# Attention scores on one core: 16 KB load runs, whole tiles to one evacuating engine, and earlier transposes

## The chip, the cores and the metric

The kernel runs on one core of a Trainium2 chip. The metric is device time in microseconds (us). The profile's span of one execution is about 1.8 us shorter than that time (204.96 with 203.2).

## The reference

```python
# q, k: float32 [8, 8, 512, 64]; result: float32 [8, 8, 512, 512]
scale = 1.0 / np.sqrt(q.shape[-1])
return (np.einsum('bhqd,bhkd->bhqk', q, k) * scale).astype(np.float32)
```

It reads 16.78 MB and writes 67.11 MB. That is 83.89 MB for 1.07 billion multiply-adds.

## The kernel before

The work is cut in four units of two batches. Each unit loads keys and queries, casts them to bf16, transposes them on TensorE so that the head dimension lies on partitions, and computes eight store tiles of 2 MB. The queries go into a tile whose other half is zero, so that one matmul over 128 partitions serves one of two heads.

```python
raw_pool = ctx.enter_context(tc.tile_pool(name="raw", bufs=4))    # 8 KB a partition each
bf_pool = ctx.enter_context(tc.tile_pool(name="bf", bufs=5))
t_pool = ctx.enter_context(tc.tile_pool(name="t", bufs=2))
out_pool = ctx.enter_context(tc.tile_pool(name="out", bufs=5))    # 16 KB a partition each
tpsum_pool = ...  # 2 PSUM tiles for transposes; psum_pool: 3 for scores
# ... load_and_cast(v): four 1 MB loads a unit, in 8 KB runs
            for x in range(2):
                xf = raw_pool.tile([P, R * D], f32, name="xf")
                nc.sync.dma_start(out=xf, in_=src[v, x])
# ... transpose(v, kb, qb): after eight transposes into tp, both engines take half of it
            for x in range(2):
                for h in range(2):
                    copy = (nc.vector.tensor_copy, nc.scalar.copy)[h]
                    copy(out=kT[half(h), x * N:(x + 1) * N, :, j0:j0 + 8],
                         in_=tp[half(x)].rearrange("d j (n h m) -> d h n m j", n=N, h=2)[:, h])
# ... scores(v, c, kT, qz): 4 x (two matmuls, one eviction on ScalarE or VectorE), one 2 MB store
# ... the order
    ts = {0: transpose(0, *cast[0])}
    for v in range(UNITS):
        for c in range(C):
            scores(v, c, *ts[v])
            if c == C // 2 - 1 and v + 1 < UNITS:
                ts[v + 1] = transpose(v + 1, *cast[v + 1])
```

## Time and profile before

| | before |
|---|---|
| time, median | 204.4 us |
| span of the profiled run | 203.2 us |
| TensorE / VectorE / ScalarE busy | 52% / 63% / 52% |
| mean rate over the span | 413 GB/s |
| mean rate of slices 1 to 7 (loads) | 422 GB/s |
| mean rate of slices 9 to 37 (stores) | 430 GB/s |

Read the DMA row of the slices first (the prediction shows it): it is full from the second slice on, so the question for any change is whether it lets the queue of transfers run empty, or makes a byte cheaper. Then read how far ahead of the transfers the stores are issued. The view of the output tensor gives the times from issue to landing, the list of waits what the two evacuating engines wait for (total us, times, longest):

```profile
DMA to landing us min/median/max: 12.9/20.5/23.2
```

```profile
ACT kT L99 <- DVE kT L99: 11.6, 11, 4.6
ACT qz L110 <- DVE qz L110: 11.4, 15, 1.6
```

A landing of 20.5 us is four store tiles of 4.9 us each in the queue, a landing of 12.9 us fewer than three. ScalarE loses 23.0 us in all to VectorE on the transposed tiles, but neither engine is the bound.

### The profile page before, as it was taken

What the parts mean: (1) busy time and instruction counts of PE and PEld (TensorE: products, weight loads), DVE (VectorE), ACT (ScalarE), POOL (GpSimd) and SP (SyncE); (2) the same over time, 40 slices, a digit from 0 to 9 for tenths busy, and PEclk for the clock granted to TensorE, in tenths of its full rate; (3) what the DMA queues carried; (4) which work ended last, traced back from release to release, by engine and by line L of the source; (5) the groups of instructions that cost most, each with busy time, mean ns of one, the idle gap of its engine ahead of it and who ended that gap; (6) DMA issues with size and microseconds to landing.
All of it is one profiled execution on the core that took longest, in us unless ns stands there. A gap on an engine that the chain in (4) does not pass through costs nothing.

```text
span 203.2 us, 1530 instructions
## 1 busy us (share of the span) xinstructions
PE 105.0 (52%) x512; PEld 48.5 (24%) x512; DVE 128.3 (63%) x131; ACT 104.8 (52%) x131; POOL 34.8 (17%) x21
## 2 busy tenths in 40 slices
PE   0033579873388535979555938545455755610000
PEld 0033334332352213533122413112121211200000
DVE  3793778997769989779678889444444444440000
ACT  2317668866676867688384787333333333330000
POOL 8957777706000000000000000000000000000000
PEclk9999999999559999699988699997975597575555
DMA  6999999999999999999999999999999999999990
GB/s 226 427 411 429 421 426 423 419 424 426 432 435 426 435 423 423 439 429 426 435 432 423 435 426 432 435 423 439 429 424 435 426 429 435 429 429 439 423 419 35
DMA packets 6919, 83.98 MB, mean 413 GB/s; under 512 B 768, under 2 KB 768, under 8 KB 768
## 3 DMA queue, kind: packets, MB, share of 16 engines
q1 hardware_dynamic: 6912, 83.89, 97.3%
q8 instruction: 4, 0.07, 0.1%
q14 instruction: 3, 0.02, 0.0%
HBM read 16.78 MB, written 67.11 MB: 413 GB/s over the span
## 4 chain that ended last, share of the span: by engine, by line
DMA 42%; DVE 17%; PE 15%; ACT 13%; issue 1%; SPq 0%; ACTq 0%
DMA out_dram<-o 38%; PE ps L121 9%; DVE o L60 8%; ACT o L58 6%; DMA xf<-in_q_dram 4%; DVE kT L99 4%; ACT kT L99 4%; PE tp L105 4%; DVE qz L110 3%; PE tp L94 3%; ACT qz L110 2%; DVE xb L76 2%; ACT xb L76 1%; SPq L71 0%; ACTq L58 0%
## 5 line engine op out<-in xcount | busy, mean ns | idle before, releaser
L121 PE MATMUL ps<-kT,qz 128*128 128x512 bf16 x256 | 82.3, 450 | 38.2 <-ACT o L58 30.6
L60 DVE TENSOR_SCALAR o<-ps 128x1024 f32<-128x1024 f32 x64 | 77.5, 1223 | 36.2 <-DMA out_dram<-o 22.1
L58 ACT ACTIVATE o<-ps 128x1024 f32<-128x1024 f32 x64 | 63.2, 1022 | 40.7 <-DMA out_dram<-o 34.7
L121 PEld LDWEIGHTS <-qz 128*128 128x128 bf16 x256 | 27.3, 109 | 86.7 <-issue 70.4
L99 ACT COPY kT<-tp 64x512 bf16<-64x512 bf16 x32 | 18.4, 579 | 15.6 <-DVE kT L99 11.6
L110 DVE COPY qz<-tp 64x512 bf16<-64x512 bf16 x32 | 21.5, 686 | 6.5 <-PE tp L105 6.2
L76 POOL CAST xb<-xf 128x2048 bf16<-128x2048 f32 x12 | 22.7, 1893 | 15.5 <-PE tp L94 7.0
L94 PE MATMUL tp<-identity,xb 128*128 128x128 bf16 x128 | 12.5, 261 | 24.0 <-ACT kT L99 11.1
L110 ACT COPY qz<-tp 64x512 bf16<-64x512 bf16 x32 | 18.2, 579 | 12.1 <-DVE qz L110 11.4
L99 DVE COPY kT<-tp 64x512 bf16<-64x512 bf16 x32 | 21.3, 684 | 5.0 <-PE tp L94 4.4
L105 PE MATMUL tp<-identity,xb 128*128 128x128 bf16 x128 | 12.4, 263 | 12.6 <-ACT kT L99 7.3
L94 PEld LDWEIGHTS <-xb 128*128 128x128 bf16 x128 | 10.9, 121 | 27.5 <-issue 16.3
L105 PEld LDWEIGHTS <-xb 128*128 128x128 bf16 x128 | 11.0, 121 | 16.6 <-issue 15.4
L85 POOL MEMSET qz<- 64x4096 bf16 x3 | 11.5, 3830 | 0.1
L76 DVE CAST xb<-xf 128x2048 bf16<-128x2048 f32 x2 | 7.2, 3604 | 3.7 <-DMA xf<-in_k_dram 2.6
L76 ACT CAST xb<-xf 128x2048 bf16<-128x2048 f32 x2 | 3.8, 1897 | 6.1 <-DMA xf<-in_k_dram 6.0
L85 DVE MEMSET qz<- 64x2048 uint32 x1 | 1.8, 1765 | 1.2 <-PEq L158 1.2
L76 ACT ACT_TABLE_LOAD x1 | 1.3, 1283 | 0.7 <-PEq L158 0.7
masks.py:199 POOL TENSOR_SCALAR_AFFINE_SELECT identity<-identity 128x128 bf16<-128x128 bf16 x1 | 0.3, 292 | 0.1
masks.py:197 POOL MEMSET identity<- 128x128 bf16 x1 | 0.2, 204 | 0.3 <-POOLq L158 0.3
L158 POOL MEMSET const-float32-0.0<- 128x1 f32 x1 | 0.1, 103 | 0.2 <-issue 0.2
L158 POOL MEMSET const-bfloat16-1.0<- 128x1 bf16 x1 | 0.1, 111 | 0.0
(2 smaller groups left out, 0.2 us busy)
## 6 DMA issues: line engine op xcount, KB each, us to landing
out_dram<-o SPq DMA_DIRECT2D x32, 2048.0 KB, 20.5
xf<-in_k_dram SPq DMA_DIRECT2D x8, 1024.0 KB, 7.9
xf<-in_q_dram SPq DMA_DIRECT2D x8, 1024.0 KB, 8.4
```

Of the source, the lines that this page charges most:

```text
L58: nc.scalar.mul(out=dst, in_=src, mul=scale)
L60: nc.vector.tensor_scalar(out=dst, in0=src, scalar1=scale, scalar2=None, op0=mybir.AluOpType.mult)
L76: copy(out=xb[:, :, x, :], in_=xf.rearrange("p (j d) -> p j d", j=R))
L85: engine.memset(qz[half(h), :, :, (1 - h) * U:(2 - h) * U], 0.0)
L94: nc.tensor.transpose(out=tp[:, j, :], identity=identity, in_=kb[:, j0 + j].rearrange("p x d -> p (x d)"))
L99: copy(out=kT[half(h), x * N:(x + 1) * N, :, j0:j0 + 8], in_=tp[half(x)].rearrange("d j (n h m) -> d h n m j", n=N, h=2)[:, h])
L105: nc.tensor.transpose(out=tp[:, i, jj, :], identity=identity, in_=qb[:, RO * jj + i0 + i].rearrange("p x d -> p (x d)"))
L110: copy(out=qz[half(h), i0:i0 + IW, x * N:(x + 1) * N, h * U:(h + 1) * U] .rearrange("d i n (m jj) -> d i n m jj", jj=JJ), in_=tp[half(x)]. ...
L121: nc.tensor.matmul(out=ps[:, w, :], lhsT=qz[:, i + w, c, :], rhs=kT[:, c].rearrange("d m j -> d (m j)"), start=True, stop=True)
L158: nc = _bacc.Bacc("TRN2", target_bir_lowering=False, num_devices=1)
```

## The change

Its intent: half as many loads with runs twice as long; no waiting of the two engines on each other in a transposed tile; and the second unit's transposes early, while loads still fill the queue. The larger load buffers take the room of one output buffer.

```diff
-    q_r = q.rearrange("(v x) g (m j) d -> v x (g m) (j d)", x=2, j=R)
+    q_r = q.rearrange("(v b) g (m j) d -> v (b g m) (j d)", b=2, j=R)
 # ... k_r, out_r alike
-    raw_pool = ctx.enter_context(tc.tile_pool(name="raw", bufs=4))
+    raw_pool = ctx.enter_context(tc.tile_pool(name="raw", bufs=3))
-    out_pool = ctx.enter_context(tc.tile_pool(name="out", bufs=5))
+    out_pool = ctx.enter_context(tc.tile_pool(name="out", bufs=4))
 # ... load_and_cast
-            for x in range(2):
-                xf = raw_pool.tile([P, R * D], f32, name="xf")
-                nc.sync.dma_start(out=xf, in_=src[v, x])
+            xf = raw_pool.tile([P, 2, J * D], f32, name="xf")
+            nc.sync.dma_start(out=xf, in_=src[v])
 # ... the evacuation of a transposed tile
+    def rearrange(tp, pattern, dst):
+        nonlocal n_tp
+        copy = (nc.vector.tensor_copy, nc.scalar.copy)[n_tp % 2]
+        n_tp += 1
+        for s in range(2):
+            src = tp[half(s)].rearrange(pattern, n=N, h=2)
+            for h in range(2):
+                copy(out=dst(s, h), in_=src[:, h])
 # ... the order
-            if c == C // 2 - 1 and v + 1 < UNITS:
+            if n == (1 if v == 0 else N // 2 - 1) and v + 1 < UNITS:
```

## The prediction

> **What bounds the kernel now.** I read the page's slices first (its part 2), then the queue table (part 3), then the windows at the hand-over from loads to stores and at the end, then the chain of waits. The slices decide most of it:
>
> ```profile
> span 203.2 us, 1530 instructions
> ...
> PE   0033579873388535979555938545455755610000
> ...
> DVE  3793778997769989779678889444444444440000
> ACT  2317668866676867688384787333333333330000
> ...
> DMA  6999999999999999999999999999999999999990
> GB/s 226 427 411 429 421 426 423 419 424 426 432 435 426 435 423 423 439 429 426 435 432 423 435 426 432 435 423 439 429 424 435 426 429 435 429 429 439 423 419 35
> ...
> q1 hardware_dynamic: 6912, 83.89, 97.3%
> q8 instruction: 4, 0.07, 0.1%
> ```
>
> A slice is 203.2/40 = 5.08 us. The DMA row stands at 9 from the second slice to the last but one, while no compute engine is full for long. So the transfers are the bound, and not by a chain of waits but by bytes: 83.89 MB must pass (16.78 read, 67.11 written). The GB/s row gives two rates. Slices 1 to 7 are loads: mean 2956/7 = 422 GB/s. Slices 9 to 37 are stores: mean 430. Loads take 16.78/0.422 = 39.8 us, stores 67.11/0.430 = 156.1 us, together 195.9 us; the other 7 us of the span are the first issue, the ramp and the end. The end is worth a look in the windows view (length, busy time of PE, PEld, DVE, ACT, POOL, clock, DMA share, GB/s):
>
> ```profile
> 38.00:40.00 2.00, 1.71 (x8) 0.60 (x7) 2.00 (x2) 1.46 (x3) 1.62 (x1) 1.00 1.00 414
> 40.00:42.00 2.00, 1.85 (x7) 0.57 (x6) 1.97 (x3) 1.85 (x2) 0.27 (x1) 1.00 0.99 381
> ...
> 199.00:200.00 1.00, 0.00 (x0) 0.00 (x0) 0.00 (x0) 0.00 (x0) 0.00 (x0) 0.50 0.04 16
> 200.00:201.00 1.00, 0.00 (x0) 0.00 (x0) 0.00 (x0) 0.00 (x0) 0.00 (x0) 0.50 0.08 33
> ```
>
> A DMA share of 0.04 to 0.08 is about one engine of sixteen: for the last 2 to 3 us one engine finishes alone. Adding up the two-microsecond windows, 16.66 MB have moved by 42.0 us, so the loads end at 42.3 us; the hand-over costs no more than the 381 shows. From there a 2.10 MB store tile keeps the queue busy 2.10/0.430 = 4.9 us. The kernel is slower only if a tile is not issued by the time its predecessor's data is out.
>
> How near that is, the chain of waits tells (start, length, what):
>
> ```profile
> 85.33 0.02 SPq L125
> ...
> 85.38 12.88 DMA out_dram<-o
> ...
> 107.93 20.24 DMA out_dram<-o
> ```
>
> The eleventh tile was issued at 85.3 us and landed 12.9 us later. Its own data is 4.9 us and I allow 1.3 us for issue and receipt (an estimate), so some 6.5 us of stores were still queued ahead: that is the smallest lead anywhere. The next, at 107.9 us, had over 13 us.
>
> **What the Trainium skill says.** "DMA: Bandwidth & Descriptors", Where 436 GB/s comes from, puts the ceiling of one core at 435 GB/s; the stores' 430 agrees, so no rearrangement of engines can make them faster. Its section Why small descriptors are slow counts about 3 extra cycles per packet, where a cycle carries 32 bytes, and 32 bytes of descriptor. For an 8 KB run, if it goes as one packet, that is 3 on 256 cycles and 32 on 8192 bytes. The loads are indeed 1.8% below the stores here, but direction and size are mixed in this difference. "PSUM — Partial Sum Buffer", PSUM bank collisions raise a hardware error, has two engines reading the same bank and quadrant kept apart by a dependency. This trace agrees (timeline, start and length first):
>
> ```profile
> 23.34 0.68 DVE L110 COPY qz<-tp 64x512 bf16<-64x512 bf16 x1 [1.10 <-PE tp L105]
> ...
> 24.06 0.58 ACT L110 COPY qz<-tp 64x512 bf16<-64x512 bf16 x1 [1.21 <-DVE qz L110]
> ...
> 27.44 1.87 PE L105 MATMUL tp<-identity,xb 128*128 128x128 bf16 x16 [0.86 <-ACT qz L110]
> ```
>
> ScalarE begins its copy from the tile only when VectorE's 0.68 us on the same half are over, so a tile's four copies take three in a row, some 2.1 us.
>
> **The change part by part.**
>
> Loads: 16 of 1 MB in 8 KB runs become 8 of 2 MB in 16 KB runs; same bytes. An estimate from the skill's section: 39.8 us x (3/256 - 3/512 + 32/8192 - 32/16384) = 0.3 us saved. If the whole gap of 422 to 430 came from run length, 39.8 - 39.0 = 0.8 us. All of this lies on the bound. The load buffers hold 3 x 2 MB instead of 4 x 1 MB, so more is queued; the fourth load goes when the first is cast, at about 12 us (landed 8.0, VectorE's cast 3.8 us), and three loads keep the queue until 2.3 + 3 x 4.97 = 17.2 us. No gap.
>
> First tile: the casts start when the whole 2 MB are there, so transposes start near 12 us instead of 10.0. VectorE and ScalarE now each take four copies of their own tile, 4 x 0.69 = 2.75 us and 4 x 0.58 = 2.3 us, side by side. A pair of tiles costs one group of eight transposes (0.6 to 1.0 us) plus 2.75, so 3.4 to 3.8 us, against 4.0 before (18.32 to 22.29 us in the timeline). Gain 0.2 to 0.6 us a pair, 1 to 2 us a unit, all beside the transfers. The number of copies, transposes and matmuls and the shapes are unchanged: the output of the query copy is now in runs of 4 elements, but its source was strided already, so I keep 0.69 and 0.58 us. By my sum the first store is ready at 34 us (before: 35.7), the second at 37; neither matters before 42.3.
>
> Output buffers 5 to 4: (4 x 8 + 5 x 16) KB = (3 x 16 + 4 x 16) KB per partition, so they pay for the larger loads. This takes up to one tile, 4.9 us, from the lead.
>
> Second unit's transposes after two store tiles instead of four: now only stores 1 and 2 cover them, until 42.3 + 2 x 4.9 = 52.1 us. The built order on VectorE after these two is 8 key copies, 1 eviction, 4 query copies, 1 eviction (third tile), 4 query copies, 2 evictions (fourth). With 0.69 and 1.22 us each, 0.6 us per transposed group, and some 2 us in which TensorE's order makes it wait for a free output bank: third tile at 37 + 12 x 0.69 + 2 x 1.22 + 2 = 49.7 us, needed by 52.1 - 1.2 = 50.9. Fourth: + 4 x 0.69 + 2 x 1.22 + 1 = 55.9, needed by 55.8. So the margin at these two is about nothing: 0 to 2 us of empty queue. For the third unit the same sum gives the eleventh tile at 88 to 90 us, needed at 90.1; for the fourth, 2 to 4 us of margin.
>
> Sum: 204.4 - 0.3 (run length) + 0.4 (empty queue, an estimate weighted over 0 to 2 us) = 204.5 us.
>
> **The rivals.** (1) Nothing at all: the transfers are full either way, 203.9 to 204.4 us. For it: the DMA row, and equal bytes; I hold it likeliest. (2) The queue runs dry where transposes now cover only two tiles, or where one fewer output buffer is queued: 205 to 208 us. For it: the sum above has little margin, and in slices 10 and 11 before the TensorE clock fell to 0.5, which makes a group of eight transposes 1.0 us instead of 0.6. Against: the two engines now evacuate side by side without waiting on each other, and the early transposes lie beside loads. (3) Longer runs help loads by more than the estimate, or the ramp of the first 3 us is shorter as the first two megabytes go by one issue: 203.2 to 203.8 us. Against a gain over 2%: it would need 200.3 us, under the 195.9 us of data plus the start and the tail, which the change leaves alone.
>
> **Range and chances.** Low end 203.3: rival 3 with no gap. High end 206.3: about 2 us of gaps. Slower by 2% (over 208.5) needs 4 us of gaps, twice my worst sum; 0.05. Faster by 2%: 0.02. Within: 0.93.
>
> **What will show it.** The DMA row at 9 from slice 1 to 38 says rival 1; a 7 or 8, or GB/s below 400, in slices 9 to 11 (50 to 58 us) or 17 (88 us) says rival 2. The GB/s of slices 1 to 7 above 425 shows the run length worth something; 430 would show that length, not direction, was the gap. Copies of 0.69 and 0.58 us, and no ScalarE copy waiting for VectorE, show the evacuation step right. The smallest store landing time should fall from 12.9 us to 6 to 10. The prediction is wrong if the query copies grow with their 4-element runs (0.3 us on 32 copies per engine would empty the queue), or if a load waits for a cast.

## The result, and the profile after

The changed kernel takes 204.52 us (204.16 to 204.69, 4 runs) against 204.40 (204.25 to 204.78, 4 runs). The ratio is 1.0001, with a 95% interval of 0.9981 to 1.0021. A ratio here and below is the mean time of one kernel's fast runs over the mean of the other's fast runs of the same rounds, so it is not quite the ratio of the medians quoted.

The page of the changed kernel, span, slices and queue:

```profile
span 202.4 us, 1541 instructions
...
DMA  6999999999999999999999999999999999999994
GB/s 207 437 437 421 434 437 421 415 411 431 440 421 434 428 424 431 434 395 415 418 418 428 440 418 415 431 444 421 421 418 447 424 415 418 444 434 415 423 447 191
...
q1 hardware_dynamic: 5760, 83.89, 97.9%
```

The queue is as full as before. Its packets fell from 6912 to 5760: 1024 fewer for runs twice as long, which go as one packet each, and 128 fewer that end a transfer. Three things differ in the GB/s row. Slices 1 to 7 now average 428.9 instead of 422.3. Slice 17 falls to 395. And the last slice holds 191 where it held 35. Landing times and waits:

```profile
DMA to landing us min/median/max: 7.6/15.9/18.6
```

```profile
ACT qz L96 <- PE tp L113: 13.8, 6, 3.0
...
ACT kT L96 <- PE tp L105: 8.2, 4, 4.5
```

The smallest landing shrank from 12.9 to 7.6 us. ScalarE no longer waits for VectorE on a transposed tile; it now waits 22.0 us for TensorE's transposes, where it had waited 23.0 us for VectorE. The wait changed its name and hardly its size. The copies themselves kept their length (688 and 580 ns, from the page):

```profile
L96 DVE COPY qz<-tp 64x512 bf16<-64x512 bf16 x32 | 22.0, 688 | 6.5 <-PE tp L113 6.1
L96 ACT COPY qz<-tp 64x512 bf16<-64x512 bf16 x32 | 18.5, 580 | 14.2 <-PE tp L113 13.8
```

The windows around slice 17 (length, busy time of PE, PEld, DVE, ACT, POOL, clock, DMA share, GB/s) and the end:

```profile
88.00:90.00 2.00, 2.00 (x9) 0.87 (x7) 0.61 (x2) 1.28 (x2) 0.00 (x0) 0.50 0.99 426
90.00:91.00 1.00, 1.00 (x4) 0.40 (x3) 0.69 (x1) 0.63 (x1) 0.00 (x0) 0.59 0.62 262
91.00:92.00 1.00, 1.00 (x5) 0.29 (x3) 0.86 (x1) 0.89 (x2) 0.00 (x0) 1.00 0.74 311
...
199.00:200.00 1.00, 0.00 (x0) 0.00 (x0) 0.00 (x0) 0.00 (x0) 0.00 (x0) 0.50 0.70 295
200.00:201.00 1.00, 0.00 (x0) 0.00 (x0) 0.00 (x0) 0.00 (x0) 0.00 (x0) 0.50 0.12 49
```

At 90 to 92 us the queue ran out: (1 - 0.62) + (1 - 0.74) = 0.64 us of transfer time, at the eleventh store (counting the packets of the sixteen DMA engines in the trace gives 0.66). The timeline shows why: TensorE had fallen to half clock, and VectorE's eviction waited for it (the bracket is the idle time before).

```profile
88.42 3.62 PE L126 MATMUL ps<-kT,qz 128*128 128x512 bf16 x10
89.47 1.23 DVE L61 TENSOR_SCALAR o<-ps 128x1024 f32<-128x1024 f32 x1 [1.39 <-PE ps L126]
...
90.76 0.33 SPq L130 DMA_DIRECT2D out_dram<-o  x1
```

So loads became 16.78/0.4223 - 16.78/0.4289 = 0.6 us shorter by their rate, the queue lost 0.64 us, and the time did not move. The tempting story is that the two cancel. The experiments say something else.

### The profile page after: what moved, and what is told of

Read it like the earlier page. It is cut to its first block, busy times and chain, and to the rows that moved or that the text cites. A ratio compares the mean times of both kernels' runs of the same rounds, so it can differ in the third digit from the quotient of the medians.

```text
span 202.4 us, 1541 instructions
## 1 busy us (share of the span) xinstructions
PE 106.3 (53%) x512; PEld 49.1 (24%) x512; DVE 128.5 (63%) x131; ACT 104.6 (52%) x131; POOL 33.6 (17%) x21
## 3 DMA queue, kind: packets, MB, share of 16 engines
q1 hardware_dynamic: 5760, 83.89, 97.9%
HBM read 16.78 MB, written 67.11 MB: 415 GB/s over the span
## 5 line engine op out<-in xcount | busy, mean ns | idle before, releaser
L126 PE MATMUL ps<-kT,qz 128*128 128x512 bf16 x256 | 84.8, 464 | 45.7 <-ACT o L59 38.6
L126 PEld LDWEIGHTS <-qz 128*128 128x128 bf16 x256 | 28.4, 113 | 94.0 <-issue 79.9
L96 DVE COPY qz<-tp 64x512 bf16<-64x512 bf16 x32 | 22.0, 688 | 6.5 <-PE tp L113 6.1
L105 PE MATMUL tp<-identity,xb 128*128 128x128 bf16 x128 | 12.1, 250 | 24.4 <-DVE xb L80 13.1
L96 DVE COPY kT<-tp 64x512 bf16<-64x512 bf16 x32 | 22.0, 688 | 2.8 <-PE tp L105 2.3
L105 PEld LDWEIGHTS <-xb 128*128 128x128 bf16 x128 | 10.0, 113 | 28.6 <-issue 23.8
L113 PEld LDWEIGHTS <-xb 128*128 128x128 bf16 x128 | 11.3, 126 | 11.8 <-issue 8.8
L86 POOL MEMSET qz<- 64x4096 bf16 x3 | 10.5, 3508 | 0.1
L80 DVE CAST xb<-xf 128x2048 bf16<-128x2048 f32 x2 | 5.6, 2781 | 5.6 <-DMA xf<-in_k_dram 5.6
```

The source lines that it names most:

```text
L80: copy(out=xb[:, :, s, :], in_=xf[:, s].rearrange("p (j d) -> p j d", j=J))
L86: engine.memset(qz[half(h), :, :, (1 - h) * U:(2 - h) * U], 0.0)
L96: copy(out=dst(s, h), in_=src[:, h])
L105: nc.tensor.transpose(out=tp[:, j, :], identity=identity, in_=kb[:, j0 + j].rearrange("p s d -> p (s d)"))
L113: nc.tensor.transpose(out=tp[:, i, jj, :], identity=identity, in_=qb[:, RO * jj + i0 + i].rearrange("p s d -> p (s d)"))
L126: nc.tensor.matmul(out=ps[:, w, :], lhsT=qz[:, i + w, n, :], rhs=kT[:, n].rearrange("d m s j -> d (m s j)"), start=True, stop=True)
```

## The experiments

All are timed against the kernel before on the same chip; "before" had a median of 204.24 to 204.5 us in these rounds.

### Run length alone (e1_runs8k)

```diff
-            nc.sync.dma_start(out=xf, in_=src[v])
+            for s in range(2):
+                w = J * D
+                nc.sync.dma_start(out=xf[:, s], in_=src[v][:, s * w:(s + 1) * w])
```

> The changed kernel with each 2 MB load issued as two 1 MB loads in 8 KB runs, all else the same. Theory (run length is worth about 0.3 us and the transfers set the end): time 0 to 0.5 us above the changed kernel's 204.5, mean rate of slices 1 to 7 falls from 429 to about 422 to 425. Rival (the higher load rate of the changed kernel came from deeper queueing of 6 MB and not from run length): load slices stay at 428 or more and the time does not move.

Measured: 204.80 us (204.59 to 205.00), ratio to before 1.0018 (1.0006 to 1.0030). Page, GB/s row:

```profile
GB/s 223 420 433 417 424 427 417 419 425 437 433 420 437 433 420 433 433 424 433 433 427 433 430 424 437 430 424 443 427 424 440 427 422 440 430 420 443 430 417 65
```

Slices 1 to 7 are back at 422.4. So it is not the deeper queue of loads that raises the load rate, but the longer run or the larger transfer: the edit also doubles the number of loads, and no run here separates these two. Yet this run has no dip near 91 us (no window of 1 us there falls below 0.84) and is not faster: it is 0.3 us slower than the changed kernel, a difference that the two intervals do not separate.

### One output buffer more (e2_out5)

```diff
-    bf_pool = ctx.enter_context(tc.tile_pool(name="bf", bufs=5))
+    bf_pool = ctx.enter_context(tc.tile_pool(name="bf", bufs=3))
-    out_pool = ctx.enter_context(tc.tile_pool(name="out", bufs=4))
+    out_pool = ctx.enter_context(tc.tile_pool(name="out", bufs=5))
```

> The changed kernel with 5 output buffers instead of 4 (3 instead of 5 bf16 buffers make the room). The lead of the queue should grow by up to one tile, 4.9 us: smallest landing of a store rises from 7.6 to 11 us or more, and the dip at 90.5 to 91.5 us (share 0.24 to 0.31) is gone. Theory A (the gap cost its full length and cancels the loads' gain): time falls by 0.6 to 1.0 us, to 203.6. Theory B (one DMA engine lags behind the others and sets the end; it was still busy in the gap, so the gap cost little): time falls by under 0.4 us, and the end again shows one engine alone for 2 to 3 us, as before the change.

Measured: 204.31 us (204.19 to 204.72), ratio 0.9998 (0.9986 to 1.0010). Windows and landing:

```profile
90.00:91.00 1.00, 0.74 (x5) 0.36 (x4) 0.61 (x2) 1.00 (x2) 0.00 (x0) 1.00 1.08 459
91.00:92.00 1.00, 0.80 (x4) 0.22 (x3) 1.00 (x1) 0.15 (x1) 0.00 (x0) 1.00 0.96 410
```

The gap is gone, the smallest landing is 12.9 us again, loads run at 430.7 and stores at 430.3 GB/s, better than either kernel. The time is 0.2 us under the changed kernel's, within the scatter: theory B. The trace also records when each of the sixteen DMA engines reports its part of a transfer done. The spread below is the time from the first of these reports to the last. For the last store they spread over 4.2 us before the change, 1.6 us after it, and 3.6 us here. Most engines finish earlier here (fourteen by 199.9 us, where the changed kernel's first report comes at 200.0), and the last finishes as late as ever (201.5 us in both). So in the changed kernel's gap, engines that were ahead waited for engines that were behind anyway. Its own trace shows this: in the gap the DMA engines fall idle one after another, until three or four still work, and the spread drops from 2.7 us at the tenth store to 1.5 us at the eleventh.

### Transposes after four tiles (e3_four)

```diff
-            if n == (1 if v == 0 else N // 2 - 1) and v + 1 < UNITS:
+            if n == N // 2 - 1 and v + 1 < UNITS:
```

> The changed kernel with the second unit's transposes after four store tiles, as before the change. Theory (two tiles were enough cover, with some 4 us in hand): same time within 0.4 us; the dip near 91 us remains, as the later units are placed alike. Rival (placing them early is what keeps the queue full with only four buffers): a new gap of 1 us or more between 55 and 70 us, time up by 0.5 to 2 us.

Measured: 204.61 us (204.45 to 205.86), ratio 1.0017 (0.9999 to 1.0035). The dip near 91 us stays (shares of 0.69, 0.66 and 0.73 in the three windows from 90 to 93 us), and no window from 55 to 70 us falls below 0.80. Placing the second unit's transposes early is worth nothing that these runs can see.

### Both engines in each tile again (e4_split)

```diff
-        copy = (nc.vector.tensor_copy, nc.scalar.copy)[n_tp % 2]
-                copy(out=dst(s, h), in_=src[:, h])
+                (nc.vector.tensor_copy, nc.scalar.copy)[h](out=dst(s, h), in_=src[:, h])
```

> The changed kernel with VectorE and ScalarE each taking half of every transposed tile, as before the change. Theory: all of this lies beside the transfers, so the time is the same within 0.5 us; ScalarE's waits for VectorE come back (over 15 us in total), and the dip near 91 us moves or changes by no more than 1 us. Rival (evacuation by one engine keeps the lead up): the dip grows by 2 us or more and the time rises by 1 us or more.

Measured: 204.21 us (204.13 to 204.29), ratio 0.9989 (0.9976 to 1.0002). The waits are back:

```profile
ACT kT L95 <- DVE kT L95: 11.7, 11, 4.6
ACT qz L95 <- DVE qz L95: 10.6, 15, 1.3
```

The dip near 91 us is gone with them, and the smallest landing is 8.4 us. So one-engine evacuation was not what kept the queue full, and it is worth nothing that these runs can see.

### The transfers alone (e5_pure16, e6_pure8)

All compute was removed: loads into buffers of their own, 32 stores from one constant tile. Their outputs are wrong, which doesn't matter for the times.

```diff
+    o = consts.tile([P, RO, S], f32, name="o")
+    nc.vector.memset(o, 0.0)
+    # all loads as in the changed kernel (e5) or in the kernel before (e6), then
+    # UNITS * N times:  nc.sync.dma_start(out=out_r[v, n], in_=o...)
-    # casts, transposes, matmuls, evictions
```

> Transfers alone: the changed kernel's 8 loads in 16 KB runs into buffers of their own and its 32 stores from one constant tile; no casts, transposes or matmuls (its result is wrong on purpose). Theory (the bytes on the busiest DMA engine are the bound and nothing else costs more than about 1 us): 203.0 to 204.3 us, load slices 428 to 431, no dip. Rival (waits on compute still cost a few us somewhere in both kernels): 201.5 us or less.

> Transfers alone as the kernel before issues them: 16 loads in 8 KB runs, 32 stores from one constant tile, no compute (wrong on purpose). Theory: 0.2 to 0.6 us above the pure transfers in 16 KB runs, load slices at 422 to 424, the end within 1 us of the kernel before. Rival (run length is not worth anything by itself): equal to the pure transfers in 16 KB runs within 0.1 us.

Measured: 201.35 us in 16 KB runs (201.20 to 201.58; ratio to before 0.9855, 0.9841 to 0.9868) and 201.25 us in 8 KB runs (201.12 to 201.50; ratio 0.9850). Both expectations of the theory missed, and both rivals' numbers came. First, the transfers alone take 3 us less than either kernel. Second, run length is worth nothing in the end, although the pages show its rate (16 KB first, then 8 KB):

```profile
GB/s 207 427 430 434 434 430 427 430 401 420 443 443 427 420 427 437 443 427 420 430 443 437 424 420 434 443 434 424 420 437 443 434 420 420 440 440 434 420 420 269
```

```profile
GB/s 220 425 428 427 422 422 422 422 410 427 430 440 436 420 430 440 433 430 423 430 440 440 420 427 430 440 436 420 430 440 433 430 420 433 440 440 420 420 430 279
```

Slices 1 to 7 average 430.3 against 424.0. But the first slice has 207 against 220, and slices 8 and 9, where loads hand over to stores, have 401 and 420 against 410 and 427. Summed over slices 0 to 9 and set to the same moment, the long runs are ahead by 0.08 MB, or 0.2 us: the slower start (the ramp) and the hand-over took most of the gain back. In the real pair the same sum leaves 0.10 MB.

The window view of the 16 KB run shows how these transfers end:

```profile
197.00:198.00 1.00, 0.00 (x0) 0.00 (x0) 1.00 0.66 279
198.00:199.00 1.00, 0.00 (x0) 0.00 (x0) 1.00 0.00 0
```

(VectorE and GpSimd, clock, share, GB/s.) All DMA engines stop together before 198.0 us; the last store's reports spread over 0.8 us. No engine lags. So the 3 us of the real kernels come with their compute, though the queue of the kernel before never ran dry.

### One output buffer fewer (e7_out3)

```diff
-    out_pool = ctx.enter_context(tc.tile_pool(name="out", bufs=4))
+    out_pool = ctx.enter_context(tc.tile_pool(name="out", bufs=3))
```

> The changed kernel with 3 output buffers instead of 4. Theory (the lead is the only thing that stands between compute and the bound, one buffer is worth 4.9 us of it, and the changed kernel sits just at the edge): gaps of some 3 to 6 us near 85 to 92 us and smaller ones in the fourth unit, time 207 to 212. Rival (lagging engines hide gaps of this size too, or the lead never was the limit): under 206 us.

Measured: 207.91 us (207.52 to 208.93), ratio 1.0183 (1.0159 to 1.0206).

```profile
91.00:92.00 1.00, 0.78 (x2) 0.36 (x3) 0.00 (x0) 0.82 (x1) 0.00 (x0) 0.50 0.12 49
92.00:93.00 1.00, 1.00 (x3) 0.30 (x2) 1.00 (x1) 0.10 (x1) 0.00 (x0) 0.50 0.04 16
93.00:94.00 1.00, 1.00 (x4) 0.40 (x3) 0.46 (x2) 0.93 (x1) 0.00 (x0) 0.61 0.00 0
```

Here 0.88 + 0.96 + 1.00 = 2.8 us are empty, and 1.3 us more at 133 to 135 us. The time is 3.4 us above the changed kernel's. A gap of 0.64 us hid behind the lagging engine; gaps of 4.1 us do not. Four buffers are the edge, as the prediction's small margins said.

### Does TensorE's instruction stream cost transfer time? (e9_pure16_pe, e12_pure16_pe2, e10_pure16_evac)

The queue table of every real kernel has a line of instruction fetches: 4 packets, 0.07 MB. To e5 were added, with no transfer waiting for any of it: 512 matmuls with their weight loads (e9), 1024 of a quarter of the columns (e12), or 150 evictions on each of VectorE and ScalarE (e10). Their outputs are wrong, which doesn't matter for the times.

```diff
+    for m in range(512):        # e12: 1024, on 128 columns
+        nc.tensor.matmul(out=ps, lhsT=w[:, :P], rhs=w, start=True, stop=True)
```

```diff
+        for m in range(150):    # e10: on ScalarE and on VectorE
+            nc.scalar.mul(out=y, in_=ps, mul=scale)
```

> The transfers alone in 16 KB runs, plus 512 matmuls with their 512 weight loads on a constant tile, which no transfer waits for: as many TensorE instructions as the real kernels have (result wrong on purpose). The real kernels are 3 us slower than the transfers alone, though no gap of the queue explains it in the kernel before. Theory F (the fetches of TensorE's instructions, 4 packets of 16 KB in the queue table, fall on single DMA engines, and an engine that lags by 0.6 us or more for each sets the end): 203 to 204.3 us, and the last 2 us of the transfers show a DMA share under 0.2. Theory W (the 3 us are small waits or SBUF traffic of the evictions): 201.3 to 201.7 us, as the transfers alone.

> The transfers alone in 16 KB runs, plus 150 evictions of 128x1024 on VectorE and 150 on ScalarE into scratch tiles, which no transfer waits for (result wrong on purpose): the engines' traffic to SBUF for most of the span with few instructions. Theory F: 201.2 to 201.9 us, nearly as the transfers alone. Theory W in its form of SBUF contention: 202.5 us or more, with the GB/s of the stores below 431 while the evictions run.

> The transfers alone in 16 KB runs, plus 1024 short matmuls with 1024 weight loads: twice the TensorE instructions of the run before (128 columns each, so that they take no longer), hence 8 fetch packets of 16 KB instead of 4 (result wrong on purpose). With 4 packets the transfers took 203.28 us against 201.35 without. Theory F1 (each fetch delays one DMA engine, mostly another one each time, and only the engine that lags most counts): 203.0 to 204.2 us. Theory F2 (they all fall on the same engine): twice the excess, 205 us or more. Theory W (not the fetches but TensorE's work): 203.3 or less, as the work in columns is halved.

Measured: e9 203.28 us (202.69 to 203.94; ratio to before 0.9946, 0.9929 to 0.9962), e12 203.03 us (202.79 to 203.11; 0.9925), e10 201.49 us (201.41 to 201.86; 0.9860). Page and windows of e9 (PE, PEld, DVE, GpSimd, clock, share, GB/s):

```profile
q8 instruction: 4, 0.07, 0.1%
```

```profile
198.00:199.00 1.00, 0.00 (x0) 0.00 (x0) 0.00 (x0) 0.00 (x0) 0.50 0.19 82
199.00:200.00 1.00, 0.00 (x0) 0.00 (x0) 0.00 (x0) 0.00 (x0) 0.50 0.08 33
```

And the queue table of e12:

```profile
q8 instruction: 8, 0.13, 0.2%
```

TensorE's instructions alone, which no transfer waits for, cost 203.28 - 201.35 = 1.9 us and bring the tail of a few DMA engines back; evictions cost 0.1 us. The last store's reports spread over 2.6 us in e9 and 0.8 us in e5. The difference of 1.8 us is nearly the whole loss. In e9's trace the spread goes from 0.6 to 1.8 us at the load that is in flight when the first 16 KB fetch runs (at 26 us), and to 2.7 us where loads hand over to stores; it never comes back. Twice the fetches cost no more (1.7 us). That fits fetches that mostly fall on different engines, of which only the worst counts. It does not fit fetches that all fall on one and add up. The times alone do not separate the fetch from TensorE's work, since e12 also computes less. The packets in the traces do: during each 16 KB fetch (0.88 to 1.11 us; the 24 fetches of e9, e12, e2 and both kernels) only 15 of the 16 DMA engines carry the kernel's bytes. And in e9 the spread stays between 2.6 and 2.8 us from 50 us on, though TensorE works until 118 us. What stays open is the step of 0.9 us at e9's hand-over, at which no fetch runs.

About 1 us lies between e9 and the real kernels. In e2 the spread is 2.1 us after the first fetch, 3.1 after the hand-over, flat until an 8 KB instruction fetch at 184 us, and 3.6 after it. Against the 0.8 us of e5 that is 2.8 of the 3.0 us by which e2 is slower. In the kernel before, 1.4 us of the spread grow slowly between 78 and 148 us, and that stays unexplained.

### Two attempts at a faster version (e8_split_out5, e11_last15)

The first joins e2 and e4: five output buffers, shared tiles, 16 KB loads. The second also splits the last store, to take load off one engine:

```diff
+        last = v == UNITS - 1 and n == N - 1
+        for rows in (slice(0, 120), slice(120, P)) if last else (slice(0, P),):
+            nc.sync.dma_start(out=out_r[v, n][rows], in_=o[rows].rearrange("p i k -> p (i k)"))
```

> A candidate that should beat both: 16 KB loads, five output buffers (three bf16 buffers make the room), and each transposed tile shared by both engines as before the change. Theory: no dip at all, load slices near 429, smallest landing 13 us or more; as the busiest DMA engine sets the end, the time is 203.9 to 204.3, so 0.1 to 0.5 us under both. Rival (gap and run length add up in full): 203.3 or less.

> The candidate with five output buffers and shared tiles, whose last store goes as two transfers, one of 120 rows and one of 8 rows. By the skill's account of how a transfer is split (largest count up to 16 that divides the rows) the 120 rows use fifteen DMA engines and the 8 rows eight, so one engine carries 131 KB less and eight carry 16 KB more each. If the lagging engine is that one: the end moves forward by 1 to 2 us, 202.3 to 203.2. If it is one of the eight: 0.6 us later, 204.8. If another: same, 204.2.

Measured: e8 204.21 us (204.18 to 204.28), ratio 0.9995 (0.9981 to 1.0008): no dip, and not faster. Its smallest landing was 9.7 us, not the 13 expected. e11 207.23 us (206.79 to 207.53), ratio 1.0134 (1.0119 to 1.0150): all three of its forecasts missed. E11's interval is clear of 1. Page of e11:

```profile
GB/s 213 430 427 430 436 427 436 401 420 436 417 443 420 440 414 443 420 433 433 427 430 430 430 424 440 424 443 424 440 420 430 430 433 430 430 428 427 369 229 67
```

The packets under 512 B on its page, one for each DMA engine's completion (647 = 39 x 16 + 15 + 8), say that the 120 rows did go over fifteen engines and the 8 rows over eight. But the last 8 us moved at about 213 GB/s, half the usual rate, with single packets of up to 2.4 us where 0.61 us is normal. Why was not looked into. No version here beats both kernels beyond doubt.

## Why the prediction was right

The predicted 204.5 us is the measured 204.52, within 2% as the largest chance had it. It lies between the times of the first and the second rival, and the second's sign came too (slice 17 at 395, under 400) without its time. By its own steps:

- **The bound.** Transfers set the time: shown by the full DMA row after, by no time gained in e2, e4 and e8, and by e7, where 4.1 us of empty queue cost 3.4. "By bytes" alone was too simple: the same bytes alone take 201.3 us. The prediction saw one engine finishing alone and counted it as part of "the start and the tail, which the change leaves alone"; e5 and e9 show that some 2 us of it come with TensorE's instructions. This did not hurt, as both kernels carry the same 512 matmuls. The stores' rate was as fixed as the prediction had it: 430 GB/s before and 431 with no compute at all (e5). The section that it cites for the 435 also says that for transfers between HBM and SBUF a limit of about 358 GB/s binds; the 430 measured here contradicts that.
- **Run length.** 0.3 us expected, at most 0.8. By the rate of slices 1 to 7 it was 0.6 us; carried over the ramp and the hand-over, about 0.2 us in both pairs; in the time of the pure pair, nothing. The direction was right for the rate. The loads at 428.9 GB/s and e1 show that most of the gap of 422 to 430 was not the direction; e1 leaves open whether it was run length or transfer size. The shorter ramp that the third rival hoped for was a longer one (207 GB/s in the first slice, 226 before).
- **Casts.** The first transposes began at 13.1 us, not near 12, as VectorE's first cast took 4.35 us and not 3.8. Loads did wait for casts, the prediction's own sign of being wrong (SyncE 14.9 us for VectorE and 11.2 for GpSimd), but the queue stayed full, so this sign was set too tight.
- **Evacuation.** Copies stayed at 0.69 and 0.58 us, also with the 4-element runs, and the waits for VectorE vanished. A pair of tiles took 3.9 and 4.3 us (18.18 to 22.10 and 22.10 to 26.43 us in the timeline), not 3.4 to 3.8: ScalarE's tile comes after two groups of transposes, where the sum had one. All this stayed beside the transfers, as said, but ScalarE's waits went over to TensorE in nearly full size, which was not foreseen.
- **First stores.** Issued at 33.7 us first, where 34 was expected.
- **Third and fourth tile.** Expected at 49.7 and 55.9 us with no margin; they were ready at 46.7 and 51.9. The second tile came 1 us earlier than assumed, and the terms for waits on TensorE (2 us and 1 us) were not needed: 35.9 + 12 x 0.69 + 2 x 1.22 = 46.6. Slices 10 and 11 are full.
- **Eleventh tile.** Expected at 88 to 90 us and needed at 90.1; issued at 90.8, with a gap of 0.64 us there, and a smallest landing of 7.6 us in the stated 6 to 10.
- **The sum.** Both terms came out smaller than -0.3 and +0.4 us: the run length is worth 0.2 us or nothing, and e2, which removes the gap, gains about 0.2 us or less, while its last store ends nearly as spread out as before the change. The +0.4 was reckoned for the third and fourth tile, which had no gap; the gap came at the eleventh. The right total owes something to luck in two small terms, and nothing to the two cancelling in full.

## What to carry to other kernels

Where the DMA row is full, ask of a change only two things: does it move fewer or cheaper bytes, and does it eat the lead with which stores are issued. Count the lead in buffers, and expect nothing until it is gone, then most of every microsecond (here 0.64 us of gap cost about 0.2 us or less, 4.1 us cost 3.4). To learn what such a kernel could at most still gain, time its transfers alone: here that is 3 us, and nearly none of it lay where the change worked.

## What the Trainium skill lacked or had wrong

- "Runtime: NRT & Kernel Launch", Instruction fetch mechanics, has instructions fetched by DMA in blocks of 16 KiB and calls the cost of a block mostly hidden. The traces agree with the block (4 packets of 16 KB for 1024 TensorE instructions), but in this transfer-bound kernel it is not hidden: each fetch took one DMA engine from the transfers for about 1 us, and 4 of them came with 1.9 us on 201.35, 8 with 1.7 us.
- "DMA: Bandwidth & Descriptors", Why small descriptors are slow: the estimate from it was 0.8% between 8 KB and 16 KB runs; the load rate differed by 1.6% (422.3 and 428.9 GB/s), and the ramp and the hand-over gave most of it back, which no page says.
- "DMA: Bandwidth & Descriptors", Why a DMA increments its semaphore by 16 and not by 1, has the count of engines right (15 and 8 completions for 120 and 8 rows), but no page warns that such a split store runs at about 213 GB/s instead of 430.
- "PSUM — Partial Sum Buffer", PSUM bank collisions raise a hardware error, on engines kept apart in a bank agrees (23.0 us of ScalarE waiting for VectorE); no page says that freeing them may only move the wait, here to 22.0 us for TensorE.
